# Where the moving tiles of a decoder layer's matmuls lie in SBUF, modulo 512 bytes

## The chip, the cores and the metric

The kernel runs on one core of one Trainium2 chip, as one program. The metric is the device time of one execution in microseconds (us). Each execution does the whole layer: 512 tokens of width 1024, batch 1, float32 in and out.

## The reference, cut to what matters

One decoder layer with two mixers in parallel, a merge, and a gated feed-forward network (FFN):

```
proj = x @ w_in                      # 1024 -> 6416 columns: q_a k_a v_a r_a d_low q_b k_b v_b g_a g_b
o_a  = gated linear attention(q_a, k_a, v_a, decay(d_low)) * silu(r_a)
o_b  = sliding-window attention with sinks(rope(q_b), rope(k_b), v_b)
mix  = (sigmoid(g_a) * (o_a @ w_branch_a) + sigmoid(g_b) * (o_b @ w_branch_b)) @ w_out
h    = layer_norm(alpha * x + mix)
ffn  = (silu(h @ w_gate) * (h @ w_up)) @ w_down        # 1024 -> 2816 -> 1024
out  = layer_norm(alpha * h + ffn)
```

## The kernel before, in words

**Products.** Every large product is made of float32r matmuls (a reduced float32 that TensorE takes at a higher rate). Each operand is split into a high part (a cast, on ScalarE) and a low part (the rest, a subtraction on VectorE), and three matmuls high x high, high x low and low x high add up in PSUM. A matmul has a *stationary* operand, 128 columns that an LDWEIGHTS loads into the array, and a *moving* operand of 128, 256 or 512 columns that streams through it. While one matmul streams, the LDWEIGHTS of the next one reads its 128 columns from SBUF. Nearly every matmul has another stationary operand than the one before it.

**Stages and what moves in them.** `feat_tile` (L239) makes the input projections and the branch products: the weights `wh`, `wl` are stationary, and 512 columns of the transposed input `xh`, `xl` move (tiles `pq`, `pka`, `pqa`, `pr`, `pgb`, `pga`), or of the attention outputs `obh`, `obl` and `oah`, `oal` (`pbb`, `pba`). The values (`pva`, L435) and the output projection (`pw`, L793 and L802) have it the other way round: slices of `xh` or of the merged `mh`, `ml` are stationary, and 512 columns of the weights move. The first FFN product (`seventh`, L918; tiles `fx`, `fy`, `fz`) is a scheme of seven products for eight on halves of tokens, features and columns: sums of weight quarters are stationary, and 256 columns of one of seven operands (`A11`, `A12`, `A22`, `S1` to `S4`) move; 11 columns of tiles x 7 x 24 = 1848 matmuls. The down projection (`down`, L1059, `pdn`) has slices of `op` (the split activations) stationary and 512 columns of `w_down` moving, in 22 steps of 12 matmuls for each half of the output columns; the last token tile of the second half is done in two parts of 256 columns. Below, "wide" is a matmul with 512 moving columns, "narrow" one with 256.

**What sets the order.** The kernel is written as a stream of calls and a scheduler orders each engine's instructions once, when the program is built; on the chip each engine takes them in that order. `piece(j, k)` makes the operand of step k of down half j: ScalarE casts its high part (L1034), VectorE makes its low part (L1035). For half 0 it takes its tile from a ring, so the cast of piece k waits until the step that had the same place is done.

**Places in SBUF.** The pools lie in a stack from the left (constants, small tiles, weights, then a pool for each phase) and one from the right. All tiles that matmuls read have sizes that are multiples of 512 bytes per partition, and so are the steps between the slices that one matmul takes, so that a tile's place modulo 512 is set by the small filler tiles alone: `level` (`LEVEL` floats, left, ahead of the weights), `edge` (`EDGE` floats, at the right end) and `beside` (`BESIDE` floats, ahead of the FFN operands on the left, at the end of the second pool on the right, and at the end of the ring of `op`). "Place" below is the byte at which the moving operand begins less that of the stationary operand, modulo 512. The places before, worked out from the pools and the program's addresses: 0 for `pbb`, `pba` and the second half of `pdn`; 256 for the first half of `pdn`; 384 for `pq`, `pka`, `pqa`, `pr`, `pgb`, `pga`; 128 for `pva` and `pw`; in the FFN 64 for the products with `A11` and `A12` and 320 for those with `A22` and `S1` to `S4`. The transposes through TensorE (128 columns of the identity move) stand at 128.

Of the kernel before, what the change touches and what calls it, by code (L numbers as in the profile page):

```python
# [9 lines left out]
F32 = mybir.dt.float32  # L10
# [6 lines left out]
P = 128  # L17
# [15 lines left out]

LEVEL, EDGE, BESIDE = 32, 24, 16

C_QA, C_KA, C_VA, C_RA, C_DL = 0, 512, 1024, 2048, 3072
C_QB, C_KB, C_GA, C_GB = 3088, 4112, 4368, 5392
# [3 lines left out]
def tile_decoder_layer(  # L43
# [24 lines left out]

    const = ctx.enter_context(tc.tile_pool(name="const", bufs=1))
    small = ctx.enter_context(tc.tile_pool(name="small", bufs=6))  # L70
    level = ctx.enter_context(tc.tile_pool(name="level", bufs=1))
    level.tile([P, LEVEL], F32, tag="level", name="level")
    wpool = ctx.enter_context(tc.tile_pool(name="weights", bufs=1))
    psum = ctx.enter_context(tc.tile_pool(name="psum", bufs=4, space=bass.MemoryType.PSUM))

    def phase(name, side="left"):
        return tc.alloc_tile_pool(name=name, bufs=1, side=side, reuse_waits="tile")
# [5 lines left out]
    right = phase("xparts", "right")  # L83
# [614 lines left out]
    right = phase("merged", "right")  # L698
# [118 lines left out]
    def operand(home, name):  # L817
        return home.tile([P, 2, HK, HT], F32R, tag=name, name=name)
# [171 lines left out]
    right.release()  # L990
    right = phase("sums", "right")
    A22, S4 = [operand(right, n) for n in ("a22", "s4")]
    right.tile([P, BESIDE], F32, tag="beside", name="beside2")
    right2 = phase("sums2", "right")
    S1, S2, S3 = [operand(right2, n) for n in ("s1", "s2", "s3")]
    h22, s1, s3 = plain("h22"), plain("s1f"), plain("s3f")
# [29 lines left out]

    def piece(j, k):
        if (j, k) not in pieces:
            home, n = (tail, 8) if j else (right2, 6)
            op = home.tile([P, 2, T], F32R, tag="op", name=f"op{j}_{k}", bufs=n)  # L1030
            if not pieces:
                right2.tile([P, BESIDE], F32, tag="beside", name="beside3")
            src = acts[k // HF, k % HF]
            ACT.copy(op[:, 0], src)  # L1034
            DVE.tensor_tensor(op[:, 1], src, op[:, 0].bitcast(F32), ALU.subtract)  # L1035
            pieces[j, k] = op
        return pieces[j, k]

    for i, q in flow[4:]:
        step(i, q)  # L1040
        if (i, q) == (HF - 1, "t3"):
            right2.release()
            right2 = phase("halves", "right")
            for k in range(4):
                piece(0, k)
    ffn.release()
    tail = phase("tail")
# [14 lines left out]
    for k in range(NF):  # L1062
        w = weight(("dn", 0), k, 0, 512)
        for t in range(NT):
            down(k, t, pw[t], w, piece(0, k), k == 0, k == NF - 1)
        if gain:
            r, v, op = gain.pop(0)
            DVE.tensor_tensor(r, r, v, op)
# [5 lines left out]
    for k in range(split):  # L1074
        w = weight(("dn", 1), k, 0, 512)
        for t in range(NT):
            for ps, span in zip(pw[t], spans[t]):
                down(k, t, ps, w, piece(1, k), k == 0, False, *span)
# [51 lines left out]
```

## Time and profile before

| | us |
|---|---|
| three runs before | 865.37, 869.77, 870.14 |
| median | 869.77 |
| the profiled execution's own time | 870.17 |
| its span, first to last instruction | 868.2 |

The profile is of one execution. Busy times of TensorE overlap, since a matmul's end is modelled; how long one matmul keeps the engine is read from the distance between the starts of neighbours in a long row of them. In the chain of waits a row has its start, its length and, after the x, how many matmuls were merged into it. In the groups of instructions a row has the line, engine, operation, output and inputs, the shape, the count, and after the bar the busy time and the mean duration of one in ns.

### The profile page before, as it was taken

The numbers are of one execution on the slowest core, as the hardware profiler recorded it, in microseconds if no ns is written. First come the engines' busy times: TensorE is split into PE (matmuls) and PEld (weight loads), VectorE is DVE, ScalarE is ACT, GpSimd is POOL, SyncE is SP. The second block draws the span as 40 slices with busy tenths as digits, with TensorE's granted clock in tenths as the row PEclk, the third lists the DMA queues.
The fourth block names the chain that finished last, engine by engine and source line by source line (L and its number), as shares of the span: only waits on it lengthen the run. The fifth ranks groups of instructions, "written<-read, shape, count | busy, mean of one in ns | idle before, by whom it ended". The sixth has DMA issues, their size and how long they took to land.

```text
span 868.2 us, 12541 instructions
## 1 busy us (share of the span) xinstructions
PE 841.2 (97%) x4922; PEld 726.7 (84%) x4922; DVE 578.0 (67%) x997; ACT 401.2 (46%) x699; POOL 94.5 (11%) x102
## 2 busy tenths in 40 slices
PE   7999999999999999999999898999999999999995
PEld 7887777787888788888888788999999999888884
DVE  4898888586675623322444669987878786964447
ACT  4557565564453422122233295554545455642321
POOL 4240220021320131000123000000000000000001
PEclk9999999999999999999999999999999999999998
DMA  8423113113113223333328301244333326242202
GB/s 243 145 74 95 52 49 98 49 49 98 49 49 97 73 74 97 97 97 97 97 97 263 101 1 46 77 143 130 113 102 99 97 73 209 84 145 92 79 1 97
DMA packets 92683, 83.13 MB, mean 96 GB/s; under 512 B 4833, under 2 KB 79601, under 8 KB 92625
## 3 DMA queue, kind: packets, MB, share of 16 engines
q1 hardware_dynamic: 90480, 76.89, 29.2%
q0 software_dynamic: 1568, 4.41, 1.6%
q10 hardware_dynamic: 576, 1.05, 0.3%
q8 instruction: 38, 0.62, 0.3%
q14 instruction: 21, 0.16, 0.1%
HBM read 80.24 MB, written 2.10 MB: 95 GB/s over the span
## 4 chain that ended last, share of the span: by engine, by line
PE 91%; DVE 3%; SPq 2%; DMA 1%; issue 1%; ACT 1%; POOL 0%; POOLq 0%; DVEq 0%; ACTq 0%
PE pdn L1059 13%; PE fx L918 13%; PE fy L918 7%; PE pva L435 5%; PE pgb L239 5%; PE pq L239 5%; PE pga L239 5%; PE pr L239 5%; PE pbb L239 5%; PE pba L239 5%; PE fz L918 4%; PE pka L239 3%; PE pqa L239 3%; PE pw L802 3%; PE po L416 2%; PE pp L405 2%
## 5 line engine op out<-in xcount | busy, mean ns | idle before, releaser
L171 DVE TENSOR_TENSOR wl<-raw,wh 128x1024 fp32r<-128x1024 f32 x96 | 121.3, 1265 | 111.7 <-ACT wh L170 111.5
L170 ACT CAST wh<-raw 128x1024 fp32r<-128x1024 f32 x96 | 100.5, 1050 | 133.5 <-PE pdn L1059 34.3
L1059 PE MATMUL pdn<-wh,op 128*128 128x512 f32 (+1 forms) x396 | 110.7, 366 | 0.0
L1059 PEld LDWEIGHTS pdn<-wh,op 128*128 128x128 f32 x396 | 71.4, 189 | 12.2
L905 ACT CAST wht<-b 128x1024 fp32r<-128x1024 f32 x44 | 46.2, 1049 | 63.9 <-DVE b L896 52.9
L1059 PE MATMUL pdn<-wl,op 128*128 128x512 f32 (+1 forms) x198 | 72.0, 365 | 0.0
L918 PE MATMUL fx<-s,wht 128*128 128x256 f32 x352 | 63.4, 280 | 1.4 <-ACT wht L905 1.4
L906 DVE TENSOR_TENSOR wlt<-b,wht 128x1024 fp32r<-128x1024 f32 x44 | 53.7, 1222 | 9.9 <-ACT wht L905 9.9
L896 DVE TENSOR_TENSOR b<-b,b 128x1024 f32<-128x1024 f32 x44 | 53.5, 1220 | 5.2 <-DMA b<-in_w_ffn_up_dram 4.8
L918 PEld LDWEIGHTS fx<-s,wht 128*128 128x128 f32 x352 | 53.7, 188 | 1.8 <-ACT wht L905 1.8
L906 DVE TENSOR_TENSOR wlb<-b,whb 128x1024 fp32r<-128x1024 f32 x33 | 40.2, 1221 | 21.5 <-ACT whb L905 18.5
L918 PE MATMUL fx<-s,wlt 128*128 128x256 f32 x176 | 49.3, 281 | 1.9 <-DVE wlt L906 1.9
L905 ACT CAST whb<-b 128x1024 fp32r<-128x1024 f32 x33 | 34.5, 1050 | 31.5 <-PE fx L918 15.6
L1059 PEld LDWEIGHTS pdn<-wl,op 128*128 128x128 f32 x198 | 37.3, 188 | 6.1
L1034 ACT CAST op<-act 128x512 fp32r<-128x512 f32 x44 | 26.1, 618 | 22.4 <-PE pdn L1059 21.6
L918 PEld LDWEIGHTS fx<-s,wlt 128*128 128x128 f32 x176 | 32.9, 187 | 2.5 <-DVE wlt L906 2.3
L1035 DVE TENSOR_TENSOR op<-act,op 128x512 fp32r<-128x512 f32 x44 | 29.0, 687 | 8.8 <-ACT op L1034 8.8
L391 ACT ACTIVATE S<-S,nm 128x256 f32<-128x256 f32 (+1 forms) x64 | 30.1, 476 | 10.3 <-DVE es L388 6.1
L918 PE MATMUL fx<-a,whb 128*128 128x256 f32 x176 | 32.9, 281 | 1.8 <-ACT a L830 1.0
L918 PE MATMUL fy<-s,whb 128*128 128x256 f32 x176 | 33.1, 280 | 0.3 <-DVE s L831 0.3
L918 PE MATMUL fx<-a,wht 128*128 128x256 f32 x176 | 31.8, 280 | 0.5 <-DVE c L966 0.5
L918 PE MATMUL fy<-s,wht 128*128 128x256 f32 x176 | 32.1, 279 | 0.0
(445 smaller groups left out, 2269.4 us busy)
## 6 DMA issues: line engine op xcount, KB each, us to landing
raw<-in_w_in_dram SPq DMA_DIRECT2D x50, 512.0 KB, 3.6
b<-in_w_ffn_gate_dram SPq DMA_DIRECT2D x44, 256.0 KB, 4.0
b<-in_w_ffn_up_dram SPq DMA_DIRECT2D x44, 256.0 KB, 4.4
raw<-in_w_ffn_down_dram SPq DMA_DIRECT2D x22, 512.0 KB, 3.5
raw<-in_w_branch_b_dram SPq DMA_DIRECT2D x8, 512.0 KB, 3.3
raw<-in_w_branch_a_dram SPq DMA_DIRECT2D x8, 512.0 KB, 3.4
raw<-in_w_out_dram SPq DMA_DIRECT2D x8, 512.0 KB, 3.5
x<-in_x_dram SPq DMA_DIRECT2D x8, 256.0 KB, 6.3
```

What stands on the lines that cost most here:

```text
L170: ACT.copy(wh, raw)
L171: DVE.tensor_tensor(wl, raw, wh.bitcast(F32), ALU.subtract)
L239: PE.matmul(ps[:, n0:n1], w, d[k][:, n0:n1] if isinstance(d, list) else d[:, k, n0:n1], start=i == 0, stop=i == 3 * NK - 1)
L391: ACT.activation(S[h], S[h], AF.Exp, bias=nm[:, h : h + 1], accum_out=den[:, h : h + 1])
L435: PE.matmul(pa[c], d[:, k, cs], w, start=k == 0 and i == 0, stop=k == NK - 1 and i == 2)
L896: DVE.tensor_tensor(a, a, b, ALU.add)
L905: ACT.copy(wh, src)
L906: lows.append(DVE.tensor_tensor(wl, src, wh.bitcast(F32), ALU.subtract))
L918: PE.matmul(ps[:, n * HT : (n + 1) * HT], w[x][:, c0 : c0 + P], op[:, y, k, :], start=start and n == 0 and i == 0, stop=stop and n == 1 an ...
L1034: ACT.copy(op[:, 0], src)
L1035: DVE.tensor_tensor(op[:, 1], src, op[:, 0].bitcast(F32), ALU.subtract)
L1059: PE.matmul(ps[:, c0:c1], op[:, x, ts], w[y][:, c0:c1], start=start and n == 0, stop=stop and n == 2)
```

## The change

It takes the filler `level` out and sets `EDGE` 24, `BESIDE` 48 and `ROW` 128 floats. The weights' pool and all pools behind it on the left (weights, attention outputs, the second ring of `op`, residuals) now lie 128 bytes lower, at 384 modulo 512. `xh`, `xl`, `mh` and `ml` stay at 384. The FFN operands on the left stay at 64, those on the right move from 320 to 64. The ring of `op` for half 0 of the down projection has 5 tiles in place of 6 and lies at 384.

```diff
-LEVEL, EDGE, BESIDE = 32, 24, 16
+EDGE, BESIDE, ROW = 24, 48, 128
...
-    level = ctx.enter_context(tc.tile_pool(name="level", bufs=1))
-    level.tile([P, LEVEL], F32, tag="level", name="level")
...
-    right.tile([P, BESIDE], F32, tag="beside", name="beside2")
+    right.tile([P, ROW - BESIDE], F32, tag="beside", name="beside2")
...
-            home, n = (tail, 8) if j else (right2, 6)
+            home, n = (tail, 8) if j else (right2, 5)
```

The places after: 0 for all wide matmuls; 192 for all of the FFN; 256 for the transposes through TensorE; the small products of the attention stages stay at 0 or 256, and the narrow matmuls of the start (`pk`, `pv`, `pd`) go from 384 to 0.

No instruction is added or taken out. Up to the end of the FFN the order on every engine is the same, and so it is for the DMAs throughout. The ring moves a few instructions in the first half of the down projection. On VectorE (DVE), at the start of that half, with the names `op0_k` and `op1_k` for the pieces of half 0 and half 1, before:

```order
L1035 TENSOR_TENSOR op1_6_7723<-act0_6_6233,op1_6_7723 128x512
L1035 TENSOR_TENSOR op1_7_7741<-act0_6_6233,op1_7_7741 128x512
L1035 TENSOR_TENSOR op0_6_7286<-act0_6_6233,op0_6_7286 128x512
L1068 TENSOR_TENSOR res0_0_4128<-res0_0_4128,b1_7142 128x512
L1068 TENSOR_TENSOR res0_1_4129<-res0_1_4129,b1_7142 128x512
L171 TENSOR_TENSOR wl79_7243<-raw79_7182,wh79_7242 128x1024
L1068 TENSOR_TENSOR res1_0_4130<-res1_0_4130,b1_7142 128x512
L1035 TENSOR_TENSOR op0_7_7302<-act0_6_6233,op0_7_7302 128x512
```

and the same stretch of VectorE in the changed kernel:

```order
L1033 TENSOR_TENSOR op1_6_7719<-act0_6_6229,op1_6_7719 128x512
L1033 TENSOR_TENSOR op1_7_7737<-act0_6_6229,op1_7_7737 128x512
L1033 TENSOR_TENSOR op0_5_7260<-act0_4_5765,op0_5_7260 128x512
L1066 TENSOR_TENSOR res0_0_4124<-res0_0_4124,b1_7138 128x512
L1066 TENSOR_TENSOR res0_1_4125<-res0_1_4125,b1_7138 128x512
L169 TENSOR_TENSOR wl79_7239<-raw79_7178,wh79_7238 128x1024
L1066 TENSOR_TENSOR res1_0_4126<-res1_0_4126,b1_7138 128x512
L1033 TENSOR_TENSOR op0_6_7282<-act0_6_6229,op0_6_7282 128x512
```

The low part of piece 5, which stood right behind that of piece 4 and ahead of all `op1` pieces, now stands where that of piece 6 stood, and that of piece 6 where that of piece 7 stood. On TensorE, step 5 of the first down half before (each row is one token tile; x2 is high x high and low x high):

```order
L1059 MATMUL pdn0_0_7152<-wh76_7172,op0_5_7264 128x512 x2
L1059 MATMUL pdn0_0_7152<-wl76_7173,op0_5_7264 128x512
L1059 MATMUL pdn0_1_7153<-wh76_7172,op0_5_7264 128x512 x2
L1059 MATMUL pdn0_1_7153<-wl76_7173,op0_5_7264 128x512
L1059 MATMUL pdn0_2_7154<-wh76_7172,op0_5_7264 128x512 x2
L1059 MATMUL pdn0_2_7154<-wl76_7173,op0_5_7264 128x512
```

and the same step in the changed kernel:

```order
L1057 MATMUL pdn0_0_7148<-wh76_7168,op0_5_7260 128x512
L1057 MATMUL pdn0_1_7149<-wh76_7168,op0_5_7260 128x512
L1057 MATMUL pdn0_2_7150<-wh76_7168,op0_5_7260 128x512
L1057 MATMUL pdn0_3_7151<-wh76_7168,op0_5_7260 128x512
L1057 MATMUL pdn0_0_7148<-wh76_7168,op0_5_7260 128x512
L1057 MATMUL pdn0_0_7148<-wl76_7169,op0_5_7260 128x512
```

The four matmuls that read the high part alone now come first, and the fifth is the first that reads the low part; steps 6 and 7 are written in this way in both kernels.

## The prediction

> **What bounds the kernel now.** I read the page's first part, then the waits, the chain of waits, and the groups of instructions by shape. First the page, and TensorE's two longest waits (us in total, times, longest):
>
> ```profile
> PE 841.2 (97%) x4922; PEld 726.7 (84%) x4922; DVE 578.0 (67%) x997; ACT 401.2 (46%) x699; POOL 94.5 (11%) x102
> PE pt_x L220 <- DMA x<-in_x_dram: 3.9, 2, 3.7
> PE pw L802 <- DVE res L739: 2.4, 1, 2.4
> ```
>
> TensorE (PE) hardly waits. What counts, then, is how long one matmul holds it. In the chain of waits (start, us, piece) long rows of one kind of matmul give that:
>
> ```profile
> 28.10 5.60 PE pq L239 x24
> 137.89 7.47 PE pva L435 x32
> 155.62 4.64 PE pka L239 x20
> 192.12 5.35 PE pqa L239 x23
> 215.55 5.80 PE pr L239 x25
> 302.54 11.14 PE pgb L239 x48
> 325.72 0.87 PE pot L606 x8
> 326.59 43.56 PE pbb L239 x192
> 370.14 44.79 PE pga L239 x192
> 414.94 43.56 PE pba L239 x192
> 501.48 4.64 PE pw L802 x20
> 561.11 2.83 PE fy L918 x24
> 563.94 2.83 PE fz L918 x24
> 566.77 2.83 PE fx L918 x24
> ```
>
> Length over count: the wide matmuls take 226.9 ns in pbb and pba (43.56 / 192), at place 0, but 233.3 in pga right between them, 233.3 and 233.4 in pq and pva, and 232.0 to 232.6 in pka, pqa, pr, pgb and pw, all at places 384 or 128. The narrow ones of the FFN take 117.9 ns (2.83 / 24) at place 64 (fz) as at 320 (fy). A transpose takes 108.8 (0.87 / 8). Two more places are in the timeline of TensorE (start, us). Between the first pair of rows lie 21 wide matmuls of the first down half, place 256; between the second 33 narrow ones, place 0; between the third 11 narrow ones of the start, place 384:
>
> ```profile
> 748.38 0.39 PE L1059 MATMUL pdn<-wl,op 128*128 128x512 f32 x1
> ...
> 753.14 0.39 PE L1059 MATMUL pdn<-wl,op 128*128 128x512 f32 x1
> ...
> 853.05 0.28 PE L1059 MATMUL pdn<-wl,op 128*128 128x256 f32 x1
> ...
> 857.01 0.28 PE L1059 MATMUL pdn<-wl,op 128*128 128x256 f32 x1
> ...
> 18.92 0.28 PE L265 MATMUL pd<-xh,wd 128*128 128x256 f32 x1
> ...
> 20.22 0.28 PE L266 MATMUL pd<-xl,wd 128*128 128x256 f32 x1
> ```
>
> That is 226.7 (4.76 / 21), 120.0 (3.96 / 33) and 118.2 (1.30 / 11). So 0 and 256 agree, 128 and 384 nearly, 64 and 320 fully: what matters seems to repeat every 256 bytes. Of its quarters the narrow ones show 0, 64 and 128. **The quarter 192, to which the whole FFN goes, no row shows.**
>
> **The wide matmuls: 232 to 233 ns become 226.9.** All go to place 0, which pbb and pba show. pga gains 44.79 - 43.56 = 1.23 us. pgb, pr (192 each), pka, pqa (96 each): 576 x 5.2 ns = 3.00. The second row of pw (L802): 96 x 5.1 = 0.49. pq and pva, 384 x 6.4 = 2.46, stand in the attention stage, where VectorE is nearly as full as TensorE, and a faster TensorE may wait for it. The windows for this stage, the start of the FFN and the FFN (length, then PE, PEld, DVE, ACT, POOL busy):
>
> ```profile
> 28.00:116.00 88.00, 88.00 (x449) 68.60 (x449) 75.73 (x195) 53.16 (x133) 20.13 (x14) 1.00 0.25 73
> 511.00:552.00 41.00, 36.53 (x299) 35.17 (x297) 36.91 (x50) 24.94 (x37) 0.00 (x0) 1.00 0.21 60
> 552.00:734.00 182.00, 181.53 (x1542) 181.33 (x1540) 145.86 (x148) 94.94 (x122) 2.11 (x4) 1.00 0.38 111
> ```
>
> In the first of them VectorE is busy for 86% (75.73 / 88), so I count two thirds, 1.64. The first pw row (L793, 96 matmuls) I cost at nothing: it ends in the 2.4 us wait above, and a faster row waits longer; without that wait it would bring 0.5. pbb, pba and pdn stay. Sum 6.36; ends 4.7 (no pq and pva) and 7.7 (all of them, and L793).
>
> **Transposes through TensorE** go from 128 to 256. Durations by shape at 128 (pot) and at 0 (gs), both with 128 columns:
>
> ```profile
> L606 PE MATMUL pot<-ident,or 128*128 128x128 f32 x32 | 4.1, 272 | 0.0
> L536 PE MATMUL gs<-qs,ks 128*128 128x128 f32 x32 | 4.6, 278 | 0.0
> ```
>
> 228 of them would lose up to 6 ns, 1.4 us; not all of a duration is pace, and I take 0.3. The 128 narrow matmuls of the start lose 128 x 1.8 ns = 0.2 or nothing: nothing. Wide and transposes together: **-6.1 us**.
>
> **The narrow matmuls of the FFN: 117.9 to an unknown number.** About 1540 lie in the window 552 to 734, where TensorE leads; in the 41 us ahead of it VectorE is busy for longer than TensorE (36.91 against 36.53), and I leave its 300 out. So 1 ns is 1.54 us. The dearest narrow row is 120.0, the cheapest with a new stationary operand 108.8 (pot), where the load of 128 columns alone can set the pace. 64 and 320 are the nearest rows, each 128 bytes away, so I start from their 117.9; but below it lie 9 ns and above it 2, so I put the value 2 ns lower, at 115.9: **-3.1 us** (-14.0 at 108.8, +3.2 at 120.0). VectorE's 145.86 us still fit into the 168 us that the window would have at 109, so no other engine takes over.
>
> **The ring of 5.** In the first down half, pieces are made just in time. Timeline of VectorE (DVE) and TensorE, start, us:
>
> ```profile
> 746.38 4.90 DVE L1068 TENSOR_TENSOR res<-res,g 128x512 f32<-128x512 f32 x8
> 751.20 1.89 DVE L1035 TENSOR_TENSOR op<-act,op 128x512 fp32r<-128x512 f32 x3
> 753.00 1.29 DVE L1068 TENSOR_TENSOR res<-res,b 128x512 f32<-128x512 f32 x2
> 754.21 1.22 DVE L171 TENSOR_TENSOR wl<-raw,wh 128x1024 fp32r<-128x1024 f32 x1
> 755.34 0.69 DVE L1068 TENSOR_TENSOR res<-res,b 128x512 f32<-128x512 f32 x1
> ...
> 750.64 0.62 PE L1059 MATMUL pdn<-wh,op 128*128 128x512 f32 x2
> ...
> 753.36 1.30 PE L1059 MATMUL pdn<-wh,op 128*128 128x512 f32 x5
> ```
>
> The three subtractions from 751.20 are op1_6, op1_7 and op0_6, by the order; op0_6 is done at 753.1, and step 6 begins at 753.36. In the changed kernel op0_5 is the third of them. VectorE is one subtraction (0.6) earlier, so op0_5's low part is there at 752.5. Step 5 begins at 750.64; its four high matmuls last until 751.55; then TensorE would wait 0.9. op0_6 follows after two sums, wl79 and a sum, at 756.0; step 6, begun at 754.35, wants it at 755.3: another 0.8. Behind op0_5 on VectorE stands wl79, for step 10, and nobody waits for it yet. From step 7 on the pieces are early again. On ScalarE the casts wait for a step that is one later, with wh79 and the following ones behind them, each five pieces ahead of need: nothing. Ring: **+1.7 us** (0 to 2).
>
> **Sum.** 870.17 - 6.1 - 3.1 + 1.7 = **862.7**. The profiled execution was 0.40 above the median of the three runs (869.77), which themselves spread over 4.8; 862.7 stands for the median too.
>
> **A rule that speaks against it.** The row: pga at 384 takes 6.4 ns more than pbb and pba before and behind it, in the same loop, with the same shapes. The Trainium skill, page "TensorE: Matmul & The Clock Gate", section "Step-by-step: what each phase is for", has it that PE reads the moving operand and the next weights through two independent ports, so that loading the next weights takes no read bandwidth from the running matmul. By that rule no place could matter, and the time would be that of the rival "no effect" below; the trace disagrees by those 6.4 ns.
>
> **The rivals.** One ns of the narrow matmul decides among most, from 870.17 - 6.1 + 1.7 = 865.8 at 117.9.
> - *Forecast*, narrow at 113 to 118.5: 858.3 to 866.7. Chance 0.44 (0.36 of it below 865.4).
> - *The load of the weights alone sets the FFN's pace*: 192 lets stream and load pass each other, and the narrow matmul comes near the transpose's 108.8 to 113: 851.8 to 858.3. For it: pot shows that a load each 108.8 ns is possible; against it: three quarters show no narrow row under 117. Chance 0.24. The same page, section "LDWEIGHTS (loading the stationary operand)", gives a load of 128 columns as 128 / 1.2 = 106.7 ns; the 108.8 of pot agrees.
> - *192 is like 0, or a little worse*, 118.5 to 122: 866.7 to 872.1. For it: in a smooth cycle of four quarters opposite ones add up alike, and 120.0 + 118.2 - 117.9 is 120.3. Chance 0.15.
> - *No effect of the place*: pga is slower for something else in its stage, FFN and wide stay, the ring costs 1.7: 871.9. Against it: pbb, pga and pba follow each other with the same DMA. Chance 0.09.
> - *The ring holds the down projection up* by twice what I found, 3.4, while the rest goes as forecast: 864.4. For it: both subtractions stand behind a row of sums on a full VectorE; against it: from step 7 on there is slack. Chance 0.02.
> - *Slower*: at 192 the stream and the load meet as badly as wide ones do at 384, 6.4 ns more for each narrow matmul: 124.3, and 865.8 + 1.54 x 6.4 = 875.7. It decides from 123.3 ns on, where 0.5% is passed. For it: the FFN is the longest stage, and nothing shows its new place; against it: the narrow rows differ by 2 ns over three quarters. Chance 0.06.
>
> **How the numbers follow.** About 0.5% (4.35 us) is what a measurement can tell from no change. Faster, below 865.4: 0.36 + 0.24 + 0.02 (ring) = 0.62. Slower, above 874.1: 0.06. Same: 0.08 + 0.15 + 0.09 = 0.32. The range reaches from 852 (the cheap FFN included) to 870; outside are the slower case, no effect, and the upper part of the case like 0, about 0.2.
>
> **What would show it.** Right: pga's row of 192 at 43.6 us as pbb's; pq, pva, pgb, pr and pw at 227; pdn unchanged but for a wait of 1 to 2 us at steps 5 and 6 for op's low part; the narrow rows of 24 between 2.71 and 2.84 us. Rows of 24 at 2.62 are the second case; above 2.88 the third; at 2.98 the slower one. Wrong altogether: pga still at 44.79, or a TensorE that waits for VectorE in 28 to 150 by more than the 0.8 us that I took off.

## The result, and the profile after

The changed kernel takes 863.64 us (median of 10 runs, 861.12 to 871.69) beside 870.95 for the kernel before (10 runs, 865.37 to 873.06); the ratio is 0.9933, 95% interval [0.9903, 0.9962]. The profiled execution took 862.72, its span is 860.8 (868.2 before). The page's first part of the changed kernel:

```profile
PE 829.0 (96%) x4922; PEld 718.7 (83%) x4922; DVE 577.7 (67%) x997; ACT 401.2 (47%) x699; POOL 94.5 (11%) x102
```

The chain of waits of the changed kernel (start, us, piece) has the long rows of one kind again:

```profile
29.60 5.47 PE pq L237 x24
138.50 7.28 PE pva L433 x32
192.01 5.23 PE pqa L237 x23
301.03 10.93 PE pgb L237 x48
324.61 43.57 PE pbb L237 x192
368.18 43.52 PE pga L237 x192
411.69 43.53 PE pba L237 x192
499.57 4.56 PE pw L800 x20
618.00 2.72 PE fx L916 x24
620.72 2.72 PE fz L916 x24
634.32 2.72 PE fy L916 x24
```

Length over count: pga's 192 now take what pbb's and pba's take, 226.7 ns; pq, pva, pqa, pgb and pw 227.4 to 228.0, where 232 to 233.4 stood. The narrow rows of the FFN take 113.3 ns (2.72 / 24) in place of 117.9. The transposes lost nothing: the group pot has 272 ns, as before.

```profile
L604 PE MATMUL pot<-ident,or 128*128 128x128 f32 x32 | 4.1, 272 | 0.0
```

TensorE's waits (us in total, times, longest) in the changed kernel:

```profile
PE pw L800 <- DVE res L737: 4.7, 1, 4.7
PE pdn L1057 <- DVE op L1033: 1.4, 2, 0.9
```

The wait ahead of pw's second row has grown from 2.4 to 4.7, and the two waits for op's low parts are new. By stage, each length taken from the first matmul of one tile group to the first of the next in the two traces, in us saved:

| stretch | before | after | saved | on record |
|---|---|---|---|---|
| start, to the first pq | 27.94 | 29.44 | -1.50 | 0 |
| pq, pva and attention | 122.38 | 121.30 | 1.08 | 1.64 |
| pka, pqa, pr, pgb | 176.03 | 173.63 | 2.40 | 3.00 |
| pga | 44.79 | 43.52 | 1.27 | 1.23 |
| pw, first row and the wait behind it | 24.89 | 26.58 | -1.69 | 0 |
| pw, second row | 26.84 | 26.43 | 0.41 | 0.49 |
| FFN, its start included | 226.97 | 219.42 | 7.54 | 3.1 |
| down projection, to the first wide matmul of its second half | 61.54 | 63.56 | -2.02 | -1.7 |

pbb, pba and the second down half are unchanged to 0.02. The sum is 7.5, the spans' difference 7.4. So the time came out as forecast by terms that did not: the FFN brought 4.4 us more than its term, and the start, the pw wait, the wide rows and the ring together 4.4 us less than theirs. That these cancel is luck.

### The profile page after: what moved, and what is told of

It is laid out like the page before. It is cut to its first block, busy times and chain, and to the rows that moved or that the text cites. A ratio compares the mean times of both kernels' runs of the same rounds, so it can differ in the third digit from the quotient of the medians.

```text
span 860.8 us, 12543 instructions
## 1 busy us (share of the span) xinstructions
PE 829.0 (96%) x4922; PEld 718.7 (83%) x4922; DVE 577.7 (67%) x997; ACT 401.2 (47%) x699; POOL 94.5 (11%) x102
## 4 chain that ended last, share of the span: by engine, by line
PE 88%; DVE 5%; SPq 2%; DMA 1%; issue 1%; ACT 1%; POOL 0%; POOLq 0%; DVEq 0%; ACTq 0%
PE fx L916 12%; PE pdn L1057 11%; PE fy L916 7%; PE pva L433 5%; PE pq L237 5%; PE pr L237 5%; PE pgb L237 5%; PE pbb L237 5%; PE pba L237 5%; PE pga L237 5%; PE fz L916 3%; PE pka L237 3%; PE pqa L237 3%; PE pw L800 3%; PE po L414 2%; PE pp L403 2%
## 5 line engine op out<-in xcount | busy, mean ns | idle before, releaser
L916 PE MATMUL fx<-s,wht 128*128 128x256 f32 x352 | 61.6, 277 | 1.5 <-ACT wht L903 1.5
```

The costliest lines, as they stand in the source:

```text
L916: PE.matmul(ps[:, n * HT : (n + 1) * HT], w[x][:, c0 : c0 + P], op[:, y, k, :], start=start and n == 0 and i == 0, stop=stop and n == 1 an ...
```

## The experiments

### Each part alone

The ring by itself, on the kernel before:

```diff
-            home, n = (tail, 8) if j else (right2, 6)
+            home, n = (tail, 8) if j else (right2, 5)
```

> The kernel before with the ring of 5 alone, all places as before. Theory (the ring costs what the first down half lost, about 2.0 us, because the low parts of pieces 5 and 6 stand behind the sums on VectorE): the first down half takes 63.5 us instead of 61.5, with two waits of TensorE for op's low part of about 0.9 and 0.5 us, and the time is 2 us above the kernel before. Rival (the wait came only because the FFN ended earlier against VectorE): no such waits, the down half stays at 61.5, and the time is that of before.

873.59 (5 runs, 873.06 to 874.51), before 871.02 (15 runs); ratio 1.0032 [1.0019, 1.0045]. Its first down half takes 63.48, 1.94 more than in the kernel before (by the medians the time is 2.6 longer). So the ring costs about 2 us, with the old places as with the new ones.

The wide matmuls and the ring, on the changed kernel, with the FFN put back to 64 (left) and 320 (right):

```diff
-    ffn.tile([P, BESIDE], F32, tag="beside", name="beside")
+    ffn.tile([P, 16], F32, tag="beside", name="beside")
...
-    right.tile([P, ROW - BESIDE], F32, tag="beside", name="beside2")
+    right.tile([P, 48], F32, tag="beside", name="beside2")
...
-                right2.tile([P, BESIDE], F32, tag="beside", name="beside3")
+                right2.tile([P, 80], F32, tag="beside", name="beside3")
```

> The changed kernel with the FFN operands put back to places 64 (left) and 320 (right); wide matmuls at 0 and the ring of 5 stay. Theory (each kind of matmul is set by its own place relative to the weights): pga's row of 192 at 43.5 us as in the changed kernel, narrow rows of 24 at 2.83 us as before, so about 7.1 us are lost against the changed kernel: 870.7, within 1 us of the kernel before, since the wide gain of 5 is eaten by the ring (2.0) and the wait ahead of the second output half. Rival (the FFN got faster because its weights lie elsewhere, not because of the relative place): narrow rows stay at 2.72 and the time at 863.6.

870.09 (10 runs, 868.98 to 871.18), before 871.02; ratio 0.9988 [0.9978, 0.9997]. By the medians the wide matmuls bring 873.59 - 870.09 = 3.5 us, and the FFN's new place 870.09 - 863.64 = 6.4. pga stands at 43.52 and the wait ahead of pw's second row at 5.1 (4.7 in the changed kernel); two FFN columns take 39.57, as before.

The FFN's place and the ring, on the kernel before (`level` stays, so the wide ones stay at 384 and 128):

```diff
-    ffn.tile([P, BESIDE], F32, tag="beside", name="beside")
+    ffn.tile([P, 48], F32, tag="beside", name="beside")
...
-    right.tile([P, BESIDE], F32, tag="beside", name="beside2")
+    right.tile([P, 48], F32, tag="beside", name="beside2")
...
-                right2.tile([P, BESIDE], F32, tag="beside", name="beside3")
+                right2.tile([P, 48], F32, tag="beside", name="beside3")
```

> The kernel before with the FFN operands at place 192 and the ring of 5; weights and wide matmuls as before. Theory of the relative place: narrow rows of 24 at 2.72 us, pga's row at 44.8 us, time 7.1 below and 2.0 above the kernel before: 865.8. Rival (absolute place of the weights): narrow rows at 2.83, time 873.

866.19 (864.5 to 867.66, and one of 873.16); ratio 0.9949 [0.993, 0.9968]. The median is as expected. The profile, though, is of the execution that took 873.16, and its chain of waits shows the FFN at place 192 in the old pace:

```profile
565.02 2.83 PE fz L918 x24
567.85 2.83 PE fx L918 x24
570.67 2.83 PE fy L918 x24
```

117.9 ns, at the place where the changed kernel has 113.3. The place does not fix the pace; the next runs are about this.

### Which places, and how often

Three other pairs of places for the FFN in the changed kernel, by the same three fillers (left, right, ring): 32, 16, 112 floats for 128 and 448; 40, 72, 56 for 160 and 224; 64, none and none for 256 and 0. One run each, beside 872.47 for the kernel before.

> The changed kernel with the FFN operands on the left at place 128 and those on the right at 448 (192 + 256). Theory (the pattern repeats every 256 bytes): the rows with A11 and A12 (the first of fx, and fz) at 118 to 119 ns per matmul, as the start of the kernel before showed at 384; the rows on the right at 113.3, as at 192. Rival (512 bytes are the period, as the change's name has it): 448 is not like 192 but up to 118 or 120.

> The changed kernel with the FFN operands on the left at place 160 and those on the right at 224. Theory (what counts is a window of quarters of 64 bytes, and 192 is only the start of one): 224 at about 113 and 160 between 113 and 118. Rival (192 is a sharp best): both are 117 or more. A place cheaper than 113.3 would make a better kernel.

> The changed kernel with the FFN operands on the left at place 256 and those on the right at 0. Theory (period 256; 0 is the dearest of the places seen): both at 119 to 120 ns per matmul, as the last narrow rows of the down projection, so the FFN takes some 10 us longer than in the changed kernel and the time is 873 or 874. Rival (120 in the down projection comes from its operands, not from the place): 113 to 118.

They took 868.58, 870.38 and 875.0. At 256 and at 0 the long narrow rows of the chain of waits have 120.0 ns (2.88 / 24):

```profile
612.35 2.88 PE fx L916 x24
626.99 2.88 PE fz L916 x24
```

So for 256 and 0 the theory was right in the pace, and 1 us short in the time. At 160 and 224 a narrow matmul takes 117.8 and 118.3 ns in the mean: here the rival was right. In the run with 128 and 448 the chain of waits has this:

```profile
648.88 2.72 PE fx L916 x24
651.60 0.23 PE fy L916 x2
651.83 2.85 PE fx L916 x24
654.68 0.12 PE fy L916
654.80 2.83 PE fx L916 x24
657.62 2.71 PE fy L916 x23
```

The first row moves a right operand (448), the third a left one (128, 118.8 ns), the last three right ones again. Before the left operand 448 runs at 113.3 ns, behind it at 117.9, in one execution and in the same stage. So at 448 there are two steady rhythms, and the rhythm can change where the operand does.

All operands at one place, 64, and all at 448:

```diff
-    ffn.tile([P, BESIDE], F32, tag="beside", name="beside")
+    ffn.tile([P, 16], F32, tag="beside", name="beside")
...
-    right.tile([P, ROW - BESIDE], F32, tag="beside", name="beside2")
+    right.tile([P, 112], F32, tag="beside", name="beside2")
...
-                right2.tile([P, BESIDE], F32, tag="beside", name="beside3")
+                right2.tile([P, 16], F32, tag="beside", name="beside3")
```

(and the reverse, 112, 16, 112, for 448.)

> The changed kernel with all FFN operands at place 64 instead of 192; wide matmuls at 0 and the ring of 5 stay. Theory (192 differs from 64: at the odd multiples of 64 a narrow matmul has two steady rhythms, 113.3 and 117.8 ns, and the place sets how often it falls into which): mostly 117.8 ns, two FFN columns 39.57 us, about 870, as the run with only the wide matmuls moved (870.09, FFN at 64 and 320). Rival (what kept the kernel before out of the 113.3 ns rhythm was the switch between operands at 64 and at 320; one place for all of them lets the rhythm last): mostly 113.3 ns, columns 38.08 us, about 863.5 as the changed kernel.

> The changed kernel with all FFN operands at place 448, 256 bytes from 192; all else stays. Theory (what matters repeats every 256 bytes, so 448 is like 192): mostly 113.3 ns for a narrow matmul, FFN columns 38.08 us, about 863.5. Rival (the period is 512, and 192 is a place of its own, as 448 was not seen by itself): another pace, most likely 117.8 ns and about 870.

At 64: 870.07 (12 runs, 868.92 to 872.0), ratio 0.9987 [0.9977, 0.9998]. At 448, on the same chip: 864.05, ratio 0.9941 [0.9913, 0.9968], in two heaps: six runs from 861.9 to 864.59 and four from 869.18 to 871.76. A long row of each profile, 64 first:

```profile
612.75 2.83 PE fx L916 x24
```

```profile
614.46 2.72 PE fx L916 x24
```

So 448 is like 192, and 64 is not: the period of 256 bytes that the prediction read off holds, and the rival (it was the switch between places) falls, since 64 alone is no faster. The changed kernel's ten runs lie in two heaps too: eight from 861.12 to 865.3, and 870.06 and 871.69. Both distances are about the 7 us of the two rhythms, and the one profile of a long execution at 192, that of 873.16 above, shows the slower rhythm in its long rows.

The traces say more than the long rows. The narrow matmuls of the FFN come in stretches that end where TensorE stops for a wait or does transposes: some seven of 20 to 100 matmuls, and one of about 1580 that holds nearly all the long rows. By the distances between starts each such stretch keeps one rhythm from its first few matmuls to its end, but for the run with 128 and 448, where the rhythm changes with the operand. At 192 (six profiles) 38 of 47 stretches settle at about 113.3 ns and 9 at 117.8; at 448 6 of 8 settle at 113.3; at 64 and 320 (four profiles) 1 of 32 does. The execution of 873.16 has both rhythms at 192. Between these two rows of its timeline (start, us), in a short stretch, lie 15 matmuls at 113.3 ns, and the long stretch that begins at 548.61 has 117.8:

```profile
541.42 0.28 PE L918 MATMUL fx<-s,wlt 128*128 128x256 f32 x1
...
543.12 0.28 PE L918 MATMUL fx<-s,wlt 128*128 128x256 f32 x1
```

The one such stretch at 320 is in the profile of the kernel before, with 18 matmuls at 113.3 ns between these two rows:

```profile
530.12 0.28 PE L918 MATMUL fx<-s,wlt 128*128 128x256 f32 x1
...
532.16 0.28 PE L918 MATMUL fx<-s,wlt 128*128 128x256 f32 x1
```

So the rhythm is settled anew at the start of each stretch, and the place goes with how often it is the faster one. The long stretch alone is worth the distance of the heaps: 1578 x 4.44 ns = 7.0 us. Why one start at the same place falls into the one rhythm and the next into the other was not found.

Everything 64 bytes on (`EDGE` 8, a `level` of 16 floats), so that all distances between moving and stationary tiles stay:

> The changed kernel with the weights and all that lies behind them 64 bytes higher, and the right side moved by the same 64 bytes: all places of wide and FFN matmuls relative to each other are as in the changed kernel, but every address modulo 512 has changed (448 instead of 384); the transposes go from 256 to 192. Theory (only the difference counts): narrow 113.3, wide 226.7, time 863 to 864. Rival (absolute addresses count): either row moves by 2 ns or more.

862.83 beside 872.47, one run each. pga's row of 192 takes 43.52 us (226.7 ns) and the long stretch of the FFN 113.35 ns for a matmul, both as in the changed kernel. The addresses of weights, moving tiles and FFN operands modulo 512 have all moved and these rows have not: in this run only the distance counts.

The wide matmuls at odd multiples of 64 (`EDGE` 8; `right.tile([P, 96], ...)` keeps the FFN at 192):

> The changed kernel with the wide matmuls at odd multiples of 64 bytes: the projections at 64, values and output projection at 448 or 64, while the FFN stays at 192. Theory (for wide matmuls 0 and 256 are the best places, and any other costs): a wide matmul takes 228 to 231 ns there, between the 226.7 at 0 and the 232 to 233.4 at 128 and 384; pga's row of 192 is 43.8 to 44.4 us, and the time is 865 to 868. Rival (for wide ones too the odd multiples of 64 are best, as they are for narrow ones): under 226.7 ns, pga's row under 43.5 us, and the time under 863.

865.09 in one run. pga's row of 192:

```profile
369.84 43.96 PE pga L237 x192
```

229.0 ns at 64, and 233.3 in the mean at 448 (pva, pw): both dearer than the 226.7 at 0. For wide ones 0 (and 256, by the first down half of the kernel before) is the best of the places seen; what is best for narrow ones is not best for them.

### The two waits

The sums of the residual behind the low part of piece 6, on the changed kernel:

```diff
-    pieces = {}
+    pieces, low = {}, []
...
-            DVE.tensor_tensor(op[:, 1], src, op[:, 0].bitcast(F32), ALU.subtract)
+            low.append(DVE.tensor_tensor(op[:, 1], src, op[:, 0].bitcast(F32), ALU.subtract))
...
-        if gain:
+        if k >= 6 and gain:
...
-            DVE.tensor_tensor(r, r, v, op)
+            with tc.issue_after(low[6].ins):
+                DVE.tensor_tensor(r, r, v, op)
```

> The changed kernel with the 16 sums on the residual (gain and bias, L1068 of the kernel before) put behind the low part of piece 6 on VectorE; nothing else. Theory (the two waits of steps 5 and 6 are the low parts standing behind these sums): both waits go, the first down half takes 61.5 us, time 2.0 below the changed kernel: 861.6. Rival (a ring of 5 starves the down projection anyway): the waits move to later steps and the time stays at 863.6.

861.38 (860.06 to 862.37, and one of 867.35), ratio 0.9904 [0.9866, 0.9941]. VectorE's timeline in the changed kernel (start, us), then TensorE's around the two waits:

```profile
732.71 3.69 DVE L1033 TENSOR_TENSOR op<-act,op 128x512 fp32r<-128x512 f32 x6
736.33 4.89 DVE L1066 TENSOR_TENSOR res<-res,g 128x512 f32<-128x512 f32 x8
741.14 1.89 DVE L1033 TENSOR_TENSOR op<-act,op 128x512 fp32r<-128x512 f32 x3
742.95 1.28 DVE L1066 TENSOR_TENSOR res<-res,b 128x512 f32<-128x512 f32 x2
744.15 1.21 DVE L169 TENSOR_TENSOR wl<-raw,wh 128x1024 fp32r<-128x1024 f32 x1
745.29 0.68 DVE L1066 TENSOR_TENSOR res<-res,b 128x512 f32<-128x512 f32 x1
745.89 1.28 DVE L1033 TENSOR_TENSOR op<-act,op 128x512 fp32r<-128x512 f32 x2
```

```profile
741.10 1.07 PE L1057 MATMUL pdn<-wh,op 128*128 128x512 f32 x4
743.08 0.50 PE L1057 MATMUL pdn<-wh,op 128*128 128x512 f32 x1 [0.92 <-DVE op L1033]
745.04 1.08 PE L1057 MATMUL pdn<-wh,op 128*128 128x512 f32 x4
746.63 0.50 PE L1057 MATMUL pdn<-wh,op 128*128 128x512 f32 x1 [0.51 <-DVE op L1033]
```

op0_5 is the third of the subtractions from 741.14, behind eight sums; the fifth matmul of step 5 waits 0.92 for it, that of step 6 0.51 for op0_6. With the sums moved VectorE goes from subtraction to subtraction:

```profile
732.73 4.90 DVE L1033 TENSOR_TENSOR op<-act,op 128x512 fp32r<-128x512 f32 x8
737.55 1.22 DVE L169 TENSOR_TENSOR wl<-raw,wh 128x1024 fp32r<-128x1024 f32 x1
738.69 0.68 DVE L1033 TENSOR_TENSOR op<-act,op 128x512 fp32r<-128x512 f32 x1
739.29 4.29 DVE L1067 TENSOR_TENSOR res<-res,g 128x512 f32<-128x512 f32 x7
```

TensorE has no wait for op there, and the half takes 61.51: the ring of 5 costs nothing if the sums give way.

For the pw wait the same kernel was changed once more: the layer norm of the first output half goes ahead of the third and fourth quarters of weight sums.

```diff
-        DVE.bn_stats(stats[:, slot, :], r)
+        return DVE.bn_stats(stats[:, slot, :], r)
...
-    prep_quarters(4)
+    prep_quarters(2)
...
-        norm_part(pw[t], t, 0, st1[t], 0)
-    for i in (0, 1):
-        weight_sum(i, "t1")
+        done = norm_part(pw[t], t, 0, st1[t], 0)
+    with tc.issue_after(done.ins):
+        prep_quarters(4)
+        for i in (0, 1):
+            weight_sum(i, "t1")
```

> The changed kernel with two edits of order: the 16 sums of the residual in the down projection stand behind the low part of piece 6 (as in the run with the sums later, 861.38 beside 871.02 for the kernel before), and on VectorE the layer norm of the first half of the output projection stands ahead of the third and fourth quarters of the FFN weight sums, which had stood before it. Theory (the gain that the faster wide matmuls of the first pw row and the stages before it should have brought was given back in the wait ahead of the second pw row, 4.7 us in the changed kernel, where VectorE is late with the residual because weight sums that wait for late transfers stand ahead of it): the wait falls from 4.7 to under 1 us, the waits for low parts in the first down half are gone, and the time is about 4 us below the run with the sums later, 857 to 858. Rival (the weight sums are wanted as soon as the norm is, so that the wait only moves to the start of the FFN): the wait ahead of the second pw row is gone, but the stretch from the second pw row to the first full row of the FFN grows by as much, and the time stays at 861 to 862.

860.99 (859.73 to 861.5, and one of 867.86), ratio 0.9895 [0.9866, 0.9924]: not to be told from the 861.38 without it. The wait ahead of pw's second row is gone, and TensorE waits at the FFN's first product instead:

```profile
PE fx L916 <- ACT a L828: 4.6, 1, 4.6
```

From pw's first matmul to the first of `fx3` in the FFN it takes 112.7 us, where the run with the sums alone takes 114.3: of 4.8 us of wait 1.6 came out. The theory's 857 to 858 was wrong and the rival's mechanism nearly right. Of all kernels run these two are the fastest; both intervals lie below 1, and the changed kernel's overlaps them.

## Why the prediction was right

**Wide matmuls.** The mechanism was right: pga saved 1.27 (1.23 on record), and the second pw row 0.41 (0.49). In stages that are mixed with other work a wide matmul takes 227.4 to 228.0 rather than 226.9, and waits take a part: 2.40 for 3.00, 1.08 for 1.64. Transposes cost nothing. Together 5.2 where 6.1 was on record.

**The step that failed: "I put the value 2 ns lower, at 115.9".** It was 113.3 in the long rows: by the same 1.54 us for a ns (117.9 - 113.3) x 1.54 = 7.1, and with 0.5 in the FFN's start 7.5. The forecast case held, at its lower edge. The choice between the neighbours' 117.9 and the 108.8 of the load assumed that a place has one price, to be interpolated. It has two at 192 and at 448, and the chance of each goes with the place. The reading under it was wrong too: that three quarters show "no narrow row under 117" holds for the long rows of the chain of waits, but the same profile has a short stretch at place 320 at 113.3 ns (530.12 to 532.16, shown above). Nor did the forecast say that the kernel would have two times: two of its ten executions lie at 870 or more. The spread of the first three times of the kernel before, where 865.37 stood 4.4 us below the median, may have been a sign of it, and so may 863.54 in 15 later executions with a median of 871.02; no profile of such an execution was taken.

**The ring.** Right in place, cause and size: waits of 0.92 and 0.51 at steps 5 and 6 (0.9 and 0.8 on record), 2.0 us for the half (from start to start the two stops cost 1.19 and 0.78, with a slower first matmul behind each), and gone when the sums give way.

**The first pw row, costed at nothing: -1.69.** That a faster row only waits longer was right, but the end of the wait moved too. From pba's end to that residual, the windows (length, then PE, PEld, DVE, ACT, POOL busy, clock, DMA share, GB/s), before and after:

```profile
458.50:483.20 24.70, 22.30 (x96) 17.72 (x95) 13.31 (x13) 7.63 (x8) 5.82 (x9) 1.00 0.96 305
```

```profile
455.00:481.60 26.60, 21.97 (x97) 17.85 (x96) 13.27 (x13) 7.78 (x8) 5.82 (x9) 1.00 0.97 282
```

The same bytes (305 x 24.7 = 7.53 MB, 282 x 26.6 = 7.50) take 1.9 us longer with the DMA engines full in both. The chain of waits of the changed kernel ends in such a load and what hangs on it, with the residual behind them on VectorE:

```profile
471.93 5.51 DMA b<-in_w_ffn_up_dram
477.54 1.05 ACT whb L903
478.62 0.61 DVE wlb L904
...
479.76 1.22 DVE b L894
480.98 0.61 DVE res L737
```

So loads set this stretch, which is why a new order on VectorE gave back only 1.6 us. The wait was 2.4 to 2.7 in the three profiled kernels whose left pools lie as before (before, the ring alone, the FFN's place alone) and 3.8 to 5.1 in the ten others with this order. That the loads only look longer because TensorE comes earlier does not fit: in the run with the wide matmuls at odd multiples of 64 the left pools lie as in the changed kernel while pw's matmuls take 233.3 ns, and the stretch takes 26.36, as in the changed kernel (26.58) and not as before (24.89). That the landing place makes the loads slower fits, but no run tested it by itself; it stays open.

**The start, -1.50.** This is not the change's: the first pq begins at 27.94 in the profile of before, at 29.63 and 28.73 in the ring and the FFN runs, which start with the same program, and at 28.38 to 30.20 in the others.

**The rivals.** "The load of the weights alone" needed 113 or less; the rows stop at 113.3, close to its bound. "192 is like 0" fell: 0 has 120.0. "No effect" fell with the runs at 64, at 448 and at 256 and 0, which differ in nothing but place and lie at 870.07, 864.05 and 875.0. The ring cost 2.0, not 3.4. The slower case has no row at all: no long narrow row was dearer than 120.0 in any place tried.

## What to carry to other kernels

Where each matmul has its own load of a stationary operand, the distance of the moving from the stationary tile modulo 256 bytes is worth a sweep over its eighths, for each width apart: here it moved a wide float32r matmul between 226.7 and 233.3 ns and a narrow one between 113.3 and 120.0. (What is said of the products ahead, that nearly every matmul has another stationary operand than the one before it, does not hold for `feat_tile` and `seventh`, where one in three has the same one again; it has an LDWEIGHTS of its own all the same, 4922 for 4922 matmuls on the page.) A faster bound engine shows the next limit at once, so price each stretch that ends in a wait by what ends that wait (here loads with the DMA engines full), not by the engine that got faster. Where times of one kernel fall into two heaps, look at the pace of the longest unbroken loop in a profile of each before calling it noise, and at the short stretches too: a pace that the long rows do not show may stand there.

## What the runs showed of the hardware

- Moving operands of 256 columns at 192 or 448 bytes from the stationary ones have two steady rhythms, 113.3 and 117.8 ns. A stretch without a stop keeps one of them, the longest for some 1580 matmuls; the faster one held in 38 of 47 stretches at 192 and in 6 of 8 at 448. In the run with 128 and 448 it changes where the operand does. At 64 and 320 it held in 1 of 32, and all 22 runs of the two kernels with the wide matmuls moved and the FFN there took 868.92 or more.
- At 0 and 256 a narrow matmul takes 120.0, the dearest seen, and a wide one 226.7, the cheapest seen: the cheapest place of one width is the dearest of the other.
- 120 to 113.3 ns is 6.7, as much as the 6.6 between 233.3 and 226.7 for a matmul of twice the columns.
